# A two-layer streaming encoder on one core: the second output half of layer 0 done block by block, and the last attention queries no longer issued by force

## The chip, the core and the metric

The kernel runs on one core of one Trainium2 chip. The engines are named as in the profile: PE multiplies matrices (PEld is its weight load), DVE is the vector engine, ACT the scalar engine, POOL is GpSimd, and SP issues the transfers. The metric is the device time of one execution in microseconds (us), the median of several runs.

## What is computed

One step of an encoder with two layers over 2,048 prompt tokens and 8 samples of 16 tokens, all in float32, model width 1,024.

```python
# layer 0
z = rms_norm(h, norm_ab) @ w_in_ab      # a_q, a_k, a_v, a_g, b_qkv, b_g, b_beta, b_alpha
q, k = rms_norm per head of a_q, a_k
o_a = sliding-window attention(q, k, a_v, sinks) * silu(a_g)       # mixer A, 8 heads of 64
o_b = rms_norm(gated delta rule(conv(b_qkv), beta, g)) * silu(b_g) # mixer B, 4 heads of 128
y = h + concatenate([o_a, o_b]) @ w_out_ab
# layer 1
z = rms_norm(y, norm_c) @ w_in_c        # u and its gate, 1,024 columns each
mixed = per group of 256: ((trailing mean over 2/4/8/16) - u) @ w_grp_c * scale
out = y + (mixed * silu(gate)) @ w_out_c
```

The outputs are both hidden streams and the new caches: keys, values, delta-rule states, and histories of the convolution and of the pooled stream.

## The kernel before

**Tiles and passes.** The tokens are taken in four groups. Group 0 has four blocks of 128 prompt tokens and the block of the samples; groups 1 to 3 have four blocks each, 512 tokens. A group runs through both layers before the next begins. Every operand of a product is a pair of a high part and a low part, and one product takes three matmuls (high x high, low x high, high x low): L702 to L704 where a weight stands and the tokens stream past (`proj_fm`), L1281 to L1283 where a block of tokens stands (`tok_major`), L733 to L735 in `out_half`.

**Weights.** The plan of weights is a list. `weight()` hands out the next one and loads up to two ahead into three buffers called `w`, of 1 MB each (L448, a transfer from SP, `w<-wk`). In group 0 the weights come raw, into `wst`, and are split there: ACT casts the high part (L471), DVE and POOL subtract to get the low part (L475).

**What sets the order.** The code is one long program in which each product calls `tick(us)`. Ticks advance a planner's clock. Work is handed to that clock in three ways: `start(job)` starts a generator, which goes on each time the clock reaches the time that it yielded; `defer(DEF, fn)` issues a function 7.0 ticks later; and `queue` holds generators that are taken in turn. `finish(job)` runs a job to its end at once, `flush()` issues everything that is pending at once, and `drain()` empties the queue. What is issued is then ordered on each engine by the framework's scheduler, and each engine works through its own order.

**The last queries ahead of the gates.** `a_queries(jp)` (L1336 ff.) makes the attention queries of half the heads. For each block it makes a product with `tok_major`, normalizes it per head on ACT, DVE and POOL (`head_norm`; its last step is POOL's multiplication L1304/L1305, after POOL's power, L501), and defers `qcols`: four PE transposes into a `tp` tile (L1388), an ACT scaling (L1390) and a DVE subtraction (L1392). Behind the last block, `end` starts `a_attend(jp)` (L1396), whose four units per group make scores on PE (L1445, L1446), a row maximum on DVE, exponentials and scaling on ACT (`soft`, L1415 and L1423), transposes (L1459) and the product with the values (L1474 to L1476). After `a_queries(1)` come `drain()` and `flush()` (L1629, L1630), which issue whatever is pending, then `gates_early(0)` and `gates(1)`, both made of projections.

**The output of layer 0.** `out_half` is called twice per group in layer 0: first for the heads of half 0, then for half 1. Of a call there are four steps, two output halves `c` by two weights `kk`. The second call is `out_half(ops1, y1, normed, True)`: the first output half goes weight by weight over all blocks, the second block by block with two weights held. After a block's last product DVE adds it to the residual (L756), and `normed(b)` normalizes the row for layer 1: `norm_rows` (L537 ff.) squares one half on ACT (L526) and one on DVE (L528), POOL makes the power (L501), DVE scales (L545). After every second block a `cols` job goes into the queue: `norm_cols` (L547 ff.) transposes eight column tiles of two blocks on PE (L557), ACT casts the high part (L560), DVE subtracts for the low part (L561). The `tp` tiles have two buffers. `drain()` after the call issues what is left of it.

**The pool layer.** For the first group of channels (`gi == 0`) two weights of `u` are held, and each is taken in two halves of the tokens (matmuls of 256 columns); the two weights of the gate follow over all tokens at once (512 columns).

Of the kernel before, what the change touches and what calls it, by code (L numbers as in the profile page):

```python
# [9 lines left out]
AF = mybir.ActivationFunctionType  # L10
# [227 lines left out]
def hybrid_kernel(  # L238
# [138 lines left out]
    def flush():  # L377
        while pend:
            pend.pop(0)[1]()
# [300 lines left out]
    def group(gix, norm_job):  # L680
# [43 lines left out]
            drop(a)  # L724
            return [(h[:, i, 0:n], lo[:, i, 0:n]) for i in range(2)], [h, lo]

        def out_half(ops, y1, done=None, by_block=False):

            def products(pp, b, kk, wt):
                tk = slice(P * b, P * b + P)  # L730
                for k in range(2):
                    oh, ol = ops[2 * kk + k]
                    mm(pp, oh[:, tk], wt[0][:, k, :], start=(kk == k == 0), stop=False)  # L733
                    mm(pp, oh[:, tk], wt[1][:, k, :], start=False, stop=False)  # L734
                    mm(pp, ol[:, tk], wt[0][:, k, :], start=False, stop=(kk == k == 1))  # L735
                    tick(0.64)

            for c in range(2):

                if c and by_block:  # L740
                    ws = [weight() for _ in range(2)]
                    seq = [(b, kk, ws[kk]) for b in range(nb) for kk in range(2)]
                else:
                    seq = [(b, kk, None) for kk in range(2) for b in range(nb)]
                open_ = {}
                for b, kk, wt in seq:
                    if wt is None:
                        if b == 0:
                            cur = weight()
                        wt = cur  # L750
                    if kk == 0:
                        open_[b] = psum(("pj", "pj", "rc", "rc", "sc")[b])
                    products(open_[b], b, kk, wt)
                    if kk:
                        ysl = y1[b][:, 512 * c:512 * c + 512]
                        V.tensor_tensor(ysl, open_.pop(b), ysl, op=ALU.add)  # L756
                        if done is not None and c:
                            done(b)

        finish(norm_job)  # L760

# [864 lines left out]
                used.extend(u)  # L1626
                yield 1.2

        drain()  # L1629
        flush()  # L1630
        finish(st["B", 0], st["A", 0])
        gates_early(0)
        ops0, used0, ops1, used1 = [], [], [], []
        gs = gates(1)
        finish(st["B", 1])
# [23 lines left out]
        gain = slot([P, D])  # L1659
        Q.dma_start(gain, gains[:, D:])  # L1660

        def normed(b):
            nx[b] = slot([P, D])
            norm_rows(y1[b], nx[b], gain)
            if b % 2 or b == nb - 1:
                b0 = b - b % 2

                def cols():
                    yield 1.2
                    yield from norm_cols([nx[i] for i in range(b0, b + 1)], b0, xh, xl)  # L1670
                    drop(*[nx[i] for i in range(b0, b + 1)])

                queue.append(cols())

        out_half(ops1, y1, normed, True)
        drop(gain, *used1)
        drain()


        def pool_sums(gi, u3, ln0, su):  # L1680
# [22 lines left out]
        for gi in range(4):  # L1703
# [18 lines left out]
                uss.append(us)  # L1722

            if gi == 0:
                ws = [weight() for _ in range(2)]
                seq = [(d, w, [part]) for part in halves for d, w in enumerate(ws)]
            else:
                seq = [(d, None, None) for d in range(2)]
            for d, w, parts in seq:
                ut, ub, us = 2 * gi + d, ubs[d], uss[d]  # L1730
                for pp, t0, t1 in proj_fm(w, parts):
                    e = min(t1, Tp)
# [29 lines left out]
                    drop(pl)  # L1762

                pools.append(start(pooled(), 0.6))
            for d in range(2):
                for pp, t0, t1 in proj_fm():
                    silu2(act[:, d, t0:t1], pp)
            wh, wl = weight()
# [61 lines left out]
```

## Time and profile before

| | |
|---|---|
| median of 3 runs | 1918.76 us (1918.02 to 1921.17) |
| the profiled execution | 1920.49 us |
| its span, first to last instruction | 1918.6 us |
| PE, PEld busy | 1834.6 us (96%), 1601.5 us (83%) |
| DVE, ACT, POOL busy | 1205.8 us (63%), 722.2 us (38%), 494.6 us (26%) |
| mean granted PE clock | 0.986 of full speed |

Times in rows are microseconds from the span's start. "[2.93 <-POOL B L1305]" after an instruction means that its engine sat idle for 2.93 us before it, until POOL's write of a B tile at line 1305. In the view of waits a row gives the total, the number of times and the longest. In the view of windows PEclk is the granted clock, 1.00 for 2.4 GHz and 0.50 for 1.2 GHz.

### The profile page before, as it was taken

To read this page: it belongs to the slowest core of one execution; us is meant where nothing else is said; L and a number is where in the kernel's file an instruction comes from. 1 tells how busy PE (TensorE), PEld (TensorE's weight loads), DVE (VectorE), ACT (ScalarE), POOL (GpSimd) and SP (SyncE) were. 2 spreads that over 40 slices of the span, in tenths; PEclk is the share of its full clock that TensorE was granted. 3 is DMA by queue.
4 is the path that set the end of the run, shared out by engine and by line. 5 is a ranking of instruction groups with operands and counts; after the bars stand their busy time and mean duration, and the time that the engine had idled before them with its cause. 6 is when DMAs were issued, how large, how long until landed. Compare 5 with 4: busy or idle time off the path is not lost. (4 is left out here: it accounts for less than half of the span.)

```text
span 1918.6 us, 30851 instructions
## 1 busy us (share of the span) xinstructions
PE 1834.6 (96%) x11362; PEld 1601.5 (83%) x11362; DVE 1205.8 (63%) x3215; ACT 722.2 (38%) x1846; POOL 494.6 (26%) x628
## 2 busy tenths in 40 slices
PE   6999989999999999999999999999999999999999
PEld 5988878878997988787888988787888978787887
DVE  6797957555665697754345597664345697754342
ACT  4465336323332474441222474341222474441210
POOL 5633451423332413310012413210012413210000
PEclk9998989999999999999999999999999999999999
DMA  7433453655668533435467533435457533435454
GB/s 274 143 132 125 135 195 96 237 197 205 222 240 297 202 113 121 146 132 186 157 219 287 200 116 100 153 121 187 168 207 292 198 107 111 153 124 187 172 189 189
DMA packets 94578, 337.51 MB, mean 176 GB/s; under 512 B 35884, under 2 KB 44332, under 8 KB 64988
## 3 DMA queue, kind: packets, MB, share of 16 engines
q1 hardware_dynamic: 94428, 335.54, 50.0%
q8 instruction: 90, 1.47, 0.3%
q14 instruction: 60, 0.49, 0.1%
HBM read 256.93 MB, written 78.58 MB: 175 GB/s over the span
## 5 line engine op out<-in xcount | busy, mean ns | idle before, releaser
L702 PE MATMUL pj<-XH,w 128*128 128x512 f32 (+3 forms) x1488 | 544.1, 366 | 5.4 <-ACT cb L852 3.4
L703 PE MATMUL pj<-XL,w 128*128 128x512 f32 (+3 forms) x1488 | 534.1, 359 | 0.1
L704 PE MATMUL pj<-XH,w 128*128 128x512 f32 (+3 forms) x1488 | 533.7, 359 | 0.0
L702 PEld LDWEIGHTS pj<-XH,w 128*128 128x128 f32 x1488 | 284.1, 191 | 34.7 <-ACT cb L852 3.6
L704 PEld LDWEIGHTS pj<-XH,w 128*128 128x128 f32 x1488 | 283.5, 191 | 30.4 <-issue 0.2
L703 PEld LDWEIGHTS pj<-XL,w 128*128 128x128 f32 x1488 | 284.1, 191 | 28.9 <-issue 0.7
L475 POOL TENSOR_TENSOR w<-wst,w 128x640 fp32r<-128x640 f32 (+2 forms) x60 | 106.2, 1770 | 154.6 <-ACT w L471 150.9
L1281 PE MATMUL pj<-w,XH 128*128 128x256 f32 (+1 forms) x368 | 107.2, 292 | 0.3 <-DVE VL L1327 0.3
L1283 PE MATMUL pj<-w,XL 128*128 128x256 f32 (+1 forms) x368 | 104.7, 285 | 0.0
L1282 PE MATMUL pj<-w,XH 128*128 128x256 f32 (+1 forms) x368 | 104.5, 284 | 0.0
L756 DVE TENSOR_TENSOR A<-pj,A 128x512 f32<-128x512 f32 x40 | 27.6, 690 | 106.0 <-PE pj L735 106.0
L471 ACT CAST w<-wst 128x1024 fp32r<-128x1024 f32 (+1 forms) x60 | 61.2, 1020 | 52.5 <-PE sc L735 42.0
L715 DVE SCALAR_TENSOR_TENSOR A<-A,pj 128x512 f32<-128x512 f32 x36 | 24.7, 687 | 88.2 <-ACT A L714 88.2
L735 PE MATMUL rc<-w,B 128*128 128x512 f32 x200 | 78.0, 390 | 0.0
L735 PE MATMUL pj<-w,B 128*128 128x512 f32 x200 | 77.9, 390 | 0.0
L1688 DVE TENSOR_TENSOR B<-cb 128x526 f32<-128x526 f32 x32 | 22.7, 709 | 79.5 <-ACT cb L1733 74.3
L1281 PEld LDWEIGHTS pj<-w,XH 128*128 128x128 f32 x368 | 70.3, 191 | 1.8 <-DVE VL L1327 0.5
L1282 PEld LDWEIGHTS pj<-w,XH 128*128 128x128 f32 x368 | 70.2, 191 | 1.1 <-issue 0.5
L1283 PEld LDWEIGHTS pj<-w,XL 128*128 128x128 f32 x368 | 70.2, 191 | 0.0
L475 DVE TENSOR_TENSOR w<-wst,w 128x384 fp32r<-128x384 f32 (+2 forms) x60 | 49.1, 818 | 32.7 <-ACT w L471 32.6
L733 PE MATMUL rc<-w,B 128*128 128x512 f32 x176 | 69.4, 394 | 0.0
L733 PE MATMUL pj<-w,B 128*128 128x512 f32 x176 | 68.7, 390 | 0.0
(488 smaller groups left out, 4294.8 us busy)
## 6 DMA issues: line engine op xcount, KB each, us to landing
w<-wk SPq DMA_DIRECT2D x168, 1024.0 KB, 4.9
wk<-w SPq DMA_DIRECT2D x56, 1024.0 KB, 6.5
wst<-in_wts SPq DMA_DIRECT2D x56, 512.0 KB, 4.3
A<-in_x SPq DMA_DIRECT2D x22, 512.0 KB, 4.5
w<-wk SPq DMA_DIRECT2D x6, 1056.0 KB, 5.7
B<-in_x SPq DMA_DIRECT2D x12, 512.0 KB, 4.8
w<-wk SPq DMA_DIRECT2D x12, 512.0 KB, 3.2
out_y<-B SPq DMA_DIRECT2D x9, 512.0 KB, 3.4
```

Of the source, the lines that this page charges most:

```text
L471: S.copy(hi, st)
L475: eng.tensor_tensor(lo[:, a:b], st[:, a:b], f32(hi[:, a:b]), op=ALU.subtract)
L702: mm(pp[:, 0:w], wh[:, k, :], xh[:, k, t0:t1], start=(k == 0), stop=False)
L703: mm(pp[:, 0:w], wh[:, k, :], xl[:, k, t0:t1], start=False, stop=False)
L704: mm(pp[:, 0:w], wl[:, k, :], xh[:, k, t0:t1], start=False, stop=(k == KT - 1))
L715: V.scalar_tensor_tensor(dst, dst, 1.0, pp, op0=ALU.add, op1=ALU.mult)
L733: mm(pp, oh[:, tk], wt[0][:, k, :], start=(kk == k == 0), stop=False)
L735: mm(pp, ol[:, tk], wt[0][:, k, :], start=False, stop=(kk == k == 1))
L756: V.tensor_tensor(ysl, open_.pop(b), ysl, op=ALU.add)
L1281: mm(pp[:, 0:N], xh[:, k, tk], wh[:, k % 4, :], start=(k == 0), stop=False)
L1282: mm(pp[:, 0:N], xh[:, k, tk], wl[:, k % 4, :], start=False, stop=False)
L1283: mm(pp[:, 0:N], xl[:, k, tk], wh[:, k % 4, :], start=False, stop=(k == KT - 1))
```

## The change

There are four parts.

1. `drain()` and `flush()` no longer stand ahead of the gates; one `flush()` stands behind `gates_early(0)`. The `qcols` of the last blocks are issued when their 7 ticks are over, among the gates' projections.
2. `out_half` has a new mode, `ahead`: the first weight of the first output half goes over all blocks, then the other three weights are held together. Blocks 0 and 1 take their three remaining steps each at once, and blocks 2 and up go step by step. The third held weight goes into the buffer of the first weight.
3. In `normed` both squares are ACT's; the scaling is a started job that runs 1.9 ticks later, and the column transposes are started jobs 3.0 ticks later instead of entries of the queue. The `drain()` behind the call is gone.
4. In the pool layer at `gi == 0` three weights are held, both of `u` and the first of the gate. Each is taken in halves: all three for the first half of the tokens, which only waits for the columns of blocks 0 and 1, then all three for the second half. The gain row of the norm is dropped later.

```diff
--- before.py
+++ after.py
@@ -724,7 +724,9 @@
             drop(a)
             return [(h[:, i, 0:n], lo[:, i, 0:n]) for i in range(2)], [h, lo]
-        def out_half(ops, y1, done=None, by_block=False):
+        def out_half(ops, y1, done=None, by_block=False, ahead=False):
             def products(pp, b, kk, wt):
                 tk = slice(P * b, P * b + P)
@@ -734,6 +736,31 @@
                     mm(pp, oh[:, tk], wt[1][:, k, :], start=False, stop=False)
                     mm(pp, ol[:, tk], wt[0][:, k, :], start=False, stop=(kk == k == 1))
                     tick(0.64)
+            def add(pp, b, c):
+                ysl = y1[b][:, 512 * c:512 * c + 512]
+                V.tensor_tensor(ysl, pp, ysl, op=ALU.add)
+                if done is not None and c:
+                    done(b)
+            if ahead:
+                cur = weight()
+                open_ = {}
+                for b in range(nb):
+                    open_[0, b] = psum(("pj", "pj", "rc", "rc", "sc")[b])
+                    products(open_[0, b], b, 0, cur)
+                ws = [weight() for _ in range(3)]
+                steps = ((0, 1), (1, 0), (1, 1))
+                seq = [(b, i) for b in range(2) for i in range(3)]
+                seq += [(b, i) for i in range(3) for b in range(2, nb)]
+                for b, i in seq:
+                    c, kk = steps[i]
+                    if i == 1:
+                        open_[1, b] = psum(("sc", "pj", "pj", "rc", "rc")[b])
+                    products(open_[c, b], b, kk, ws[i])
+                    if kk:
+                        add(open_.pop((c, b)), b, c)
+                return
             for c in range(2):
@@ -752,10 +779,7 @@
                         open_[b] = psum(("pj", "pj", "rc", "rc", "sc")[b])
                     products(open_[b], b, kk, wt)
                     if kk:
-                        ysl = y1[b][:, 512 * c:512 * c + 512]
-                        V.tensor_tensor(ysl, open_.pop(b), ysl, op=ALU.add)
-                        if done is not None and c:
-                            done(b)
+                        add(open_.pop(b), b, c)
         finish(norm_job)
@@ -1626,10 +1650,9 @@
                 used.extend(u)
                 yield 1.2
-        drain()
-        flush()
         finish(st["B", 0], st["A", 0])
         gates_early(0)
+        flush()
         ops0, used0, ops1, used1 = [], [], [], []
         gs = gates(1)
         finish(st["B", 1])
@@ -1659,22 +1682,34 @@
         gain = slot([P, D])
         Q.dma_start(gain, gains[:, D:])
+        normings, colings = [], []
         def normed(b):
             nx[b] = slot([P, D])
-            norm_rows(y1[b], nx[b], gain)
+            ss = buf([P, 4, 2], "ss", 4)
+            for i in range(2):
+                junk = buf([P, 512], "t", NT)
+                S.activation(junk, y1[b][:, 512 * i:512 * i + 512], AF.Square, accum_out=ss[:, 0, i:i + 1])
+            rs = inv_rms(ss, 1)
+            def scaled():
+                yield 1.9
+                V.scalar_tensor_tensor(nx[b], y1[b], rs[:, 0:1], gain, op0=ALU.mult, op1=ALU.mult)
+            normings.append(start(scaled()))
             if b % 2 or b == nb - 1:
                 b0 = b - b % 2
-                def cols():
-                    yield 1.2
+                def cols(mine=normings[-1]):
+                    yield 3.0
+                    finish(mine)
                     yield from norm_cols([nx[i] for i in range(b0, b + 1)], b0, xh, xl)
                     drop(*[nx[i] for i in range(b0, b + 1)])
-                queue.append(cols())
-        out_half(ops1, y1, normed, True)
-        drop(gain, *used1)
-        drain()
+                colings.append(start(cols()))
+        out_half(ops1, y1, normed, ahead=True)
+        drop(*used1)
         def pool_sums(gi, u3, ln0, su):
@@ -1722,11 +1757,18 @@
                 uss.append(us)
             if gi == 0:
-                ws = [weight() for _ in range(2)]
+                ws = [weight() for _ in range(3)]
                 seq = [(d, w, [part]) for part in halves for d, w in enumerate(ws)]
             else:
                 seq = [(d, None, None) for d in range(2)]
             for d, w, parts in seq:
+                if gi == 0:
+                    finish(*(colings[0:1] if parts[0][0] == 0 else colings))
+                if d == 2:
+                    for pp, t0, t1 in proj_fm(w, parts):
+                        silu2(act[:, 0, t0:t1], pp)
+                    continue
                 ut, ub, us = 2 * gi + d, ubs[d], uss[d]
                 for pp, t0, t1 in proj_fm(w, parts):
                     e = min(t1, Tp)
@@ -1762,7 +1804,11 @@
                     drop(pl)
                 pools.append(start(pooled(), 0.6))
+            if gi == 0:
+                drop(gain)
             for d in range(2):
+                if gi == 0 and d == 0:
+                    continue
                 for pp, t0, t1 in proj_fm():
                     silu2(act[:, d, t0:t1], pp)
             wh, wl = weight()
```
**PE, around the end of `a_queries(1)`, group 1, before.** `pj_1591` is the product of the last query block, `pj_1605` the first projection of the gates; `tp_1600`, `tp_1601` and `tp_1602` are the query columns of blocks 1, 2 and 3, and `sc_1611` are scores of `a_attend(1)`.

```order
L1388 MATMUL tp_1593_8923<-first_72,B10_1559_8731 128x128 x4
...
L1283 MATMUL pj_1591_8907<-w_1536_8628,XL_75 128x256
L1388 MATMUL tp_1600_8961<-first_72,B10_1559_8731 128x128 x4
L1388 MATMUL tp_1601_8968<-first_72,B2_1560_8732 128x128 x4
L702 MATMUL pj_1605_8985<-XH_74,w_1561_8733 128x512
...
L1445 MATMUL sc_1611_8998<-KH_76,A3_1557_8729 128x256
...
L1446 MATMUL sc_1612_9005<-KL_77,A3_1557_8729 128x256
L1388 MATMUL tp_1602_8975<-first_72,B2_1560_8732 128x128 x4
L702 MATMUL pj_1605_8985<-XH_74,w_1561_8733 128x512
```
The query columns of blocks 1 and 2 stand side by side right behind the last product, the first scores three matmuls later, and block 3 behind them.

**The same place after the change.** `pj_1590` is the last query product, `pj_1601` and `pj_1614` the gates; `tp_1603`, `tp_1610` and `tp_1615` are blocks 1, 2 and 3; L1412 is L1388 before, L1469 is L1445.

```order
L1412 MATMUL tp_1592_8920<-first_72,B2_1558_8728 128x128 x4
...
L1307 MATMUL pj_1590_8904<-w_1531_8617,XL_75 128x256
L702 MATMUL pj_1601_8961<-XH_74,w_1560_8730 128x512
...
L704 MATMUL pj_1601_8961<-XH_74,w_1560_8730 128x512
L1412 MATMUL tp_1603_8971<-first_72,B2_1558_8728 128x128 x4
L702 MATMUL pj_1601_8961<-XH_74,w_1560_8730 128x512
...
L704 MATMUL pj_1601_8961<-XH_74,w_1560_8730 128x512
L1412 MATMUL tp_1610_9012<-first_72,B3_1559_8729 128x128 x4
```
Six projections stand ahead of block 1 and twelve more ahead of block 2; another six, four transposes of mixer B and six projections stand ahead of block 3 (`tp_1615`). The first score of `a_attend(1)` stands 153 rows behind the last query product, past triangular inverses of mixer B; before it stood six rows behind. In groups 2 and 3 the rows stand alike. In group 0 the columns of blocks 0 and 1 keep their place behind the same projections in both programs.

**PE, the second output half, group 1, after the change.** `w_1780` is the first weight, `w_1785`, `w_1787` and `w_1792` are the three held; `pj_1788`, `pj_1789`, `rc_1790`, `rc_1791` are the sums of the first output half of blocks 0 to 3.

```order
L737 MATMUL rc_1791_9957<-w_1780_9872,B2_1775_9824 128x512
L735 MATMUL pj_1788_9936<-w_1785_9902,B8_1777_9836 128x512
...
L735 MATMUL sc_1795_9977<-w_1787_9934,A4_1774_9823 128x512
...
L735 MATMUL pj_1789_9943<-w_1785_9902,B8_1777_9836 128x512
...
L735 MATMUL sc_1795_9977<-w_1792_9964,B8_1777_9836 128x512
...
L735 MATMUL rc_1790_9950<-w_1785_9902,B8_1777_9836 128x512
...
L557 MATMUL tp_1810_10054<-first_72,A1_1796_9991 128x128
```
Before, the four blocks of `w_1785` stood together, and only `w_1787` and `w_1792` alternated. Now `w_1792` is needed 23 matmuls behind the last use of `w_1780`, whose buffer it takes. The first transposes (`tp_1810`) stand behind 15 matmuls that follow block 1's last product; before, 9 stood between them, and the transposes of blocks 2 and 3 came behind the last product of all.

## Rows read from the trace of the kernel before

**Rows 1.** The page: busy time of the engines over the span.
```profile
PE 1834.6 (96%) x11362; PEld 1601.5 (83%) x11362; DVE 1205.8 (63%) x3215; ACT 722.2 (38%) x1846; POOL 494.6 (26%) x628
```
**Rows 2.** Waits of PE over the whole span, its first two.
```profile
PE tp L1388 <- POOL B L1305: 17.6, 10, 3.4
PE tp L557 <- DVE XL L561: 11.2, 8, 3.8
```
**Rows 3.** Timeline of group 1 at the last queries: start, duration, engine, line, operation.
```profile
776.89 0.60 PE L1388 MATMUL tp<-first,B 128*128 128x128 f32 x4
...
780.43 1.11 PE L1388 MATMUL tp<-first,B 128*128 128x128 f32 x4 [2.93 <-POOL B L1305]
...
783.68 0.61 POOL L1305 TENSOR_TENSOR B<-B,rsa 128x256 f32<-128x256 f32 x1
```
**Rows 4.** Waits of PE in 250:266, 774:786, 1200:1217 and 1636:1647, one row each.
```profile
PE tp L1388 <- POOL B L1305: 6.5, 4, 3.4
...
PE tp L1388 <- POOL B L1305: 3.2, 2, 2.9
...
PE tp L1388 <- POOL B L1305: 4.4, 3, 3.0
...
PE tp L1388 <- POOL B L1305: 3.4, 1, 3.4
```
**Rows 5.** Windows behind those waits: us, busy PE, PEld, DVE, ACT, POOL, PEclk, DMA, GB/s.
```profile
257.60:267.80 10.20, 8.18 (x34) 7.34 (x33) 6.05 (x10) 3.21 (x7) 7.74 (x10) 0.50 0.81 312
...
779.90:783.30 3.40, 2.87 (x11) 2.58 (x12) 3.27 (x8) 0.69 (x1) 1.79 (x3) 0.50 0.65 251
...
1209.90:1216.70 6.80, 5.99 (x21) 4.96 (x21) 5.79 (x15) 0.94 (x2) 3.11 (x5) 0.50 0.02 8
1640.00:1646.80 6.80, 5.65 (x21) 5.09 (x22) 5.10 (x10) 1.26 (x2) 3.25 (x5) 0.50 0.35 135
```
**Rows 6.** Window of the attention of group 0, columns as in rows 5.
```profile
287.20:320.00 32.80, 31.18 (x243) 28.23 (x242) 27.54 (x122) 25.34 (x82) 2.08 (x2) 1.00 0.26 81
```
**Rows 7.** Waits of PE in 890:920 (group 1, three rows), then in 415:450 (group 0).
```profile
PE tp L557 <- DVE XL L561: 1.5, 1, 1.5
PE tp L557 <- DVE A L545: 1.1, 1, 1.1
PE tp L557 <- DVE B L545: 0.4, 1, 0.4
...
PE tp L557 <- DVE XL L561: 2.8, 4, 1.2
PE tp L557 <- DVE B L545: 1.6, 2, 1.0
```
**Rows 8.** Timeline of group 1: matmuls of `out_half`, one block's addition and scaling.
```profile
889.72 0.39 PE L735 MATMUL rc<-w,B 128*128 128x512 f32 x1
...
894.03 0.39 PE L733 MATMUL pj<-w,B 128*128 128x512 f32 x1
...
894.90 0.69 DVE L756 TENSOR_TENSOR A<-pj,A 128x512 f32<-128x512 f32 x1 [2.03 <-PE pj L735]
...
897.45 1.28 DVE L545 SCALAR_TENSOR_TENSOR A<-A,rs,A 128x1024 f32<-128x1024 f32 x1 [0.67 <-POOL rs L501]
```
**Rows 9.** Timeline of group 1: matmuls of 256 columns in the pool layer.
```profile
916.05 0.28 PE L702 MATMUL pj<-XH,w 128*128 128x256 f32 x1
...
918.92 0.28 PE L702 MATMUL pj<-XH,w 128*128 128x256 f32 x1
```
**Rows 10.** Line L448 in 862:885: weight transfers of group 1's output.
```profile
DMA to landing us min/median/max: 4.7/4.8/6.5
```
**Rows 11.** Groups in 380:446, group 0: the split of a raw weight.
```profile
L471 ACT CAST w<-wst 128x1024 fp32r<-128x1024 f32 x8 | 8.4, 1050 | 29.2 <-PE sc L735 25.5 <-issue 3.7
...
L475 POOL TENSOR_TENSOR w<-wst,w 128x512 fp32r<-128x512 f32 x5 | 9.0, 1799 | 22.0 <-ACT w L471 22.0
```
**Rows 12.** Waits of PE in 786:846: group 1's attention, the one row.
```profile
PE sc L1057 <- ACT B L1050: 0.2, 1, 0.2
```
## The prediction

> **What bounds the kernel now.** I read the page first: PE is busy for 1834.6 us of the span and no other engine for more than 1205.8 [rows 1]. So PE sets the time, and an edit is worth what it takes out of PE's idle time or out of PE's slow stretches. The view of waits comes next. The longest wait is that of the query transposes L1388 for POOL's normalization L1305, 17.6 us, then that of the column transposes L557 of the second norm [rows 2]. Both are what the change touches.
>
> The timeline of group 1 shows how the first wait comes about. PE transposes one block's queries at 776.89 and is through at 777.49. The next transposes are already issued, by force, but POOL has not normalized that block, so PE sits for 2.93 us with projections ready behind it [rows 3]. The reader should see that it is a matter of PE's order: POOL's result for the last block ends at 783.68 + 0.61 = 784.3, 7.4 us after PE was through with its query products at 776.9, while projections that depend on nothing of this stand just behind. Split by group the wait is 6.5, 3.2, 4.4 and 3.4 us [rows 4]. Each of these is followed by a stretch at the lower clock: the granted clock is 0.50, which is 1.2 GHz, for 10.2 us in group 0 and for 3.4, 6.8 and 6.8 us in groups 1 to 3, with PE busy in them for 8.18, 2.87, 5.99 and 5.65 us [rows 5]. Before each fall PE had sat idle for 3 us or so.
>
> In the norm, PE waits 1.5 + 1.1 + 0.4 = 3.0 us in group 1 and 2.8 + 1.6 = 4.4 us in group 0 [rows 7]; groups 2 and 3 repeat group 1's three rows to 0.1 us, so groups 1 to 3 make 8.9 us. The reason is the chain behind a block's last product: DVE adds at 894.90, and the scaled row is there at 897.45 + 1.28 = 898.73 [rows 8], 3.8 us, about 4.4 with the product's own last 0.39 and the hand-over. The old order had little else for PE behind the last pair.
>
> **Part 1, no forced issue.** In groups 1 to 3 the order now has six projections ahead of block 1's query columns, twelve more ahead of block 2's, and the rest ahead of block 3's. From one matmul of 512 columns to the next it is (894.03 - 889.72) / 19 = 0.227 us [rows 8], nineteen steps lying between the two rows. Eighteen projections and one set of transposes of 0.60 us [rows 3] put block 2's at 18 x 0.227 + 0.6 = 4.7 us behind the query products; POOL's result for it came when PE went on at 780.43, 3.5 us behind them, and in groups 2 and 3 the longest waits are 0.1 and 0.5 us longer than group 1's [rows 4]. Block 3's stand at 4.7 + 0.6 + 12 x 0.227 + 0.6 (mixer B's transposes, taken as the query's) = 8.6 us, against 7.4 in group 1. So the waits of 3.2, 4.4 and 3.4 us go: **-11.0 us**, less a residual of 0.4 a group where DVE delays POOL (**+1.2**; the ends are 0 and the 11.0 itself). With the idle time goes the slow clock: half of the PE time in those three stretches, (2.87 + 5.99 + 5.65) / 2 = **-7.2 us**. In group 0 the columns of blocks 0 and 1 keep their place behind the same projections, so the wait of 6.5 us and the half of 8.18 behind it stay. I take 0; the other end is -10.6.
>
> The price is that the four attention units of the last queries are no longer begun early. Before, two were scored while DVE worked through mixer B's inverse, and PE lost only 0.2 us in all of the attention [rows 12]. Now all four run bunched behind the inverse. The trace has such a bunch, in group 0: in 32.8 us PE is busy for 31.18, DVE for 27.54 and ACT for 25.34, at clock 1.00 [rows 6]. PE idles there for 1.6 us, and I charge that to each of three groups: **+4.8**. The lower end is 0 (projections fill in), the upper end is the second rival. Group 0's own bunch was there before.
>
> The Trainium skill has a rule that speaks against this part ("TensorE: Matmul & The Clock Gate", section "A second HAM failure mode: psum-queue depth-cycling"): a PE that idles briefly and often between groups of matmuls makes the clock go back and forth between its levels. By that rule half of a bunch's 31.18 us might run at 1.2 GHz, 15.6 us more a group, and the sum would end near 1939. The trace disagrees: group 0's bunch is full of such short waits and keeps clock 1.00 [rows 6].
>
> **Parts 2 and 3, the output by blocks and the norm.** No product is added. The first pair's transposes now stand behind 15 more matmuls, 3.4 us, and a set of block 2's, where the scaled row takes 4.4; the second pair's columns are needed only by the second half of the pool layer's tokens, 72 matmuls of 256 columns after the last product. From one of these to the next it is (918.92 - 916.05) / 24 = 0.12 us [rows 9], so that is 8.6 us of cover. Of 8.9 us in groups 1 to 3 I leave 0.4 a group: **-7.7**. In group 0, with five blocks and splits on ACT and POOL, I leave 1.5 of 4.4: **-2.9**. The ends are no gain and the whole 13.3. Moving the second square from DVE to ACT costs PE nothing as long as the chain is covered so; uncovered, ACT's second square would add about the 0.69 us that DVE's took.
>
> Holding three weights costs lookahead. The third is loaded only when the first is done with, and is needed 23 matmuls later: 23 x 0.227 = 5.2 us, against a landing of 4.8 us in the median and 6.5 at worst [rows 10]. The spare in the median is 0.4 us. I take **+0.3** for three groups, from 0 to 1.3 each. In group 0 the weight has been loaded but must be split: ACT 1.05 and POOL 1.80 us [rows 11], about 3.1 with the hand-overs, behind two products of 6 x 0.227 x 2 = 2.7: **+0.5**, from 0 to 3.
>
> **Part 4, the pool layer.** The three weights go into the buffers of the three held before, in the order in which these come free. The last is free at the last product and needed 48 matmuls of 256 columns later, 5.7 us against 4.8: nothing, and 0.8 a group at the worst landing. The gate's first weight now takes 48 matmuls of 256 columns instead of 24 of 512: 48 x 0.12 = 5.7 for 5.4 us, so 0.23 a group: **+0.7** in all. The gain row dropped later costs a buffer, not time.
>
> **Sum.** -11.0 - 7.2 + 1.2 + 4.8 - 7.7 - 2.9 + 0.3 + 0.5 + 0.7 = -21.3 us. The profiled execution took 1920.5 us, 1.7 above the median of the runs; from it the sum gives 1899.2, and from the median of 1918.8 it gives **1897.5**.
>
> **The rivals.**
> - *The wait moves but half of it stays.* If DVE, busy with the inverse, delivers the sums of squares to POOL a few us later than now, the transposes still come before their data. For it: the waits end at POOL's last step, but POOL itself idles before that. Against it: nothing is put ahead of these sums on DVE. Half of 11.0 and 7.2 given back makes 9.1: 1906.6.
> - *Slower: the bunch is limited by the softmax.* ACT and DVE work in order, and ACT needs 25.34 / 4 = 6.3 us for a unit [rows 6]. If PE had other work for only 3.8 us of these, it would wait 2.5 us four times, 10 us a group, and lose the clock behind as in rows 5, 7.2 / 3 = 2.4 us. That is 12.5 for 1.6 a group: 1897.5 - 4.8 + 37.5 = 1930. It decides from (21.3 + 4.8) / 3 = 8.7 us a group. For it: the early scores are gone, and unlike in group 0 the two layers' other waits are short, so any new one shows. Against it: group 0's own bunch, and the gates' projections that stand between its matmuls.
> - *Better: group 0 gains too and the bunch is free.* Without the 4.8, and with group 0's 10.6: 1882. Against it: group 0's order at that place is nearly unchanged.
>
> That the change doesn't do what it says applies to group 0 alone, and is in the sum.
>
> **How the numbers follow.** A measurement of this kernel can tell about 0.2%, 3.8 us, from no change. I give the forecast 0.68, the first rival 0.15, the slower one 0.11 (of it 0.07 above 1922.6 and 0.03 within 0.2%), the better one 0.06. Of the first rival 0.02 may end within 0.2%. So faster is 0.88, the same 0.05, slower 0.07. The range goes from 1882, the better rival, to 1911, the first rival with the worst landings (3 x 1.3); it leaves out the slower rival and the tails, less than 0.2.
>
> **What would show it.** Right: in the view of waits L1388 for POOL falls from 17.6 to about 8, nearly all in group 0; the windows behind the queries of groups 1 to 3 show PEclk 1.00, and only group 0 keeps a stretch at 0.50; L557's waits fall to some 3 us; a wait on a weight's transfer in `out_half` is under 0.5 us a time. Wrong: PE waiting for ACT or DVE at the scores, transposes or value products of `a_attend(1)` for more than 3 us a group, or a new stretch at clock 0.50 there or at the third held weight.

## The result and the profile after

The changed kernel takes 1899.91 us in the median (1898.98 to 1901.78), against 1919.28 us (1918.02 to 1921.17) before in the same measurement: 19.4 us less, ratio 0.9898 with a 95% interval of 0.9885 to 0.991. The prediction was 1897.5, with a range of 1882 to 1911. The profiled execution of the changed kernel took 1898.98 us and has a span of 1897.2, 21.4 us under that of before.

The page's busy times of the changed kernel answer to [rows 1], and the first waits of PE over the whole span to [rows 2]. Lines have moved: L1412 is L1388 before, L1329 is L1305, L1287 is L1263, L1697 is the scaling L545.

```profile
PE 1824.5 (96%) x11434; PEld 1598.7 (84%) x11434; DVE 1196.4 (63%) x3184; ACT 733.8 (39%) x1883; POOL 498.8 (26%) x628
...
PE tp L592 <- POOL rs L501: 11.2, 4, 8.3
PE tp L1412 <- POOL B L1329: 6.0, 3, 3.4
PE tp L1412 <- DVE A L1416: 5.6, 3, 1.9
PE tp L557 <- DVE A L1697: 4.6, 6, 1.1
...
PE tp L557 <- DVE B L1697: 2.2, 2, 1.9
...
PE tp L1287 <- DVE A L1416: 2.0, 3, 0.7
```

The wait for POOL has fallen from 17.6 to 6.0 us, and what is left of it is group 0's. A new pair stands in its place: 5.6 + 2.0 us for DVE's line L1416. The wait of L557 for DVE's subtraction (11.2 us) is down to the 3.8 of the start of the kernel, and waits for the scaling L1697 remain, 4.6 + 2.2 us.

The windows at the queries answer to [rows 5]; columns as there. The second row is another place, the norm of group 0.

```profile
256.70:263.50 6.80, 5.24 (x23) 4.80 (x22) 4.80 (x8) 2.52 (x6) 6.49 (x8) 0.50 0.98 398
...
434.20:437.60 3.40, 3.40 (x18) 3.40 (x17) 2.48 (x3) 0.98 (x2) 0.21 (x1) 0.50 0.81 336
...
776.00:785.00 9.00, 6.46 (x34) 4.87 (x33) 8.57 (x20) 1.98 (x3) 2.45 (x3) 1.00 0.41 152
...
1200.00:1210.00 10.00, 7.42 (x38) 5.66 (x37) 9.53 (x22) 1.98 (x3) 2.44 (x4) 1.00 0.45 167
1624.00:1634.00 10.00, 7.53 (x38) 5.72 (x37) 9.50 (x21) 2.21 (x4) 3.54 (x5) 1.00 0.58 211
```

Group 0 still has a stretch at clock 0.50, of 6.8 us instead of 10.2. It has a new one besides, of 3.4 us behind the 1.9 us that PE waits at the norm's column transposes; before there was none at that place. In groups 1 to 3 there is none: PEclk is 1.00, though PE idles for 2.5 us in each of these windows.

Where the time went, by stage, from the starts of the first query columns of the second half (L1388, now L1412) and of the first output product (L733, now L735) to the last output product of the pool layer:

| stage | queries to output, before | after | output to end of pool layer, before | after |
|---|---|---|---|---|
| group 0 | 253.0 to 371.5 = 118.5 | 252.2 to 368.1 = 115.9 | 371.5 to 624.0 = 252.5 | 368.1 to 618.9 = 250.8 |
| group 1 | 775.0 to 858.4 = 83.4 | 769.9 to 851.3 = 81.4 | 858.4 to 1052.7 = 194.3 | 851.3 to 1044.3 = 193.0 |
| group 2 | 1202.5 to 1288.7 = 86.2 | 1194.4 to 1275.7 = 81.3 | 1288.7 to 1483.7 = 195.0 | 1275.7 to 1469.2 = 193.5 |
| group 3 | 1635.1 to 1720.1 = 85.0 | 1619.6 to 1700.1 = 80.5 | 1720.1 to 1913.4 = 193.3 | 1700.1 to 1892.0 = 191.9 |

The first stage lost 2.6 + 2.0 + 4.9 + 4.5 = 14.0 us, the second 1.7 + 1.3 + 1.5 + 1.4 = 5.9. The other 1.5 us lie in stages that the change leaves alone.

### The profile page after: what moved, and what is told of

It reads as the page before. It is cut to its first block, busy times and chain, and to the rows that moved or that the text cites. A ratio compares the mean times of both kernels' runs of the same rounds, so it can differ in the third digit from the quotient of the medians.

```text
span 1897.2 us, 30999 instructions
## 1 busy us (share of the span) xinstructions
PE 1824.5 (96%) x11434; PEld 1598.7 (84%) x11434; DVE 1196.4 (63%) x3184; ACT 733.8 (39%) x1883; POOL 498.8 (26%) x628
## 4 chain that ended last, share of the span: by engine, by line
PE 74%; DVE 16%; POOL 3%; issue 3%; ACT 2%; DMA 2%; SPq 0%; DVEq 0%; POOLq 0%; ACTq 0%
PE pj L702 12%; PE pj L704 12%; PE pj L703 12%; PE pj L737 3%; PE pj L735 3%; PE pj L736 3%; PE rc L737 2%; PE rc L735 2%; PE rc L736 2%; DVE tm L1019 2%; DVE A L1020 2%; PE pj L1305 2%; PE pj L1306 2%; PE pj L1307 2%; PE tp L557 1%
## 5 line engine op out<-in xcount | busy, mean ns | idle before, releaser
L702 PEld LDWEIGHTS pj<-XH,w 128*128 128x128 f32 x1512 | 288.2, 191 | 33.7 <-ACT cb L876 3.7
L704 PEld LDWEIGHTS pj<-XH,w 128*128 128x128 f32 x1512 | 287.5, 190 | 29.3 <-issue 0.2
L703 PEld LDWEIGHTS pj<-XL,w 128*128 128x128 f32 x1512 | 288.0, 190 | 26.5 <-issue 0.2
L1305 PE MATMUL pj<-w,XH 128*128 128x256 f32 (+1 forms) x368 | 106.8, 291 | 0.3 <-DVE VL L1351 0.3
L737 PE MATMUL pj<-w,B 128*128 128x512 f32 x224 | 87.5, 391 | 0.0
L737 PE MATMUL rc<-w,B 128*128 128x512 f32 x212 | 82.6, 390 | 0.0
L715 DVE SCALAR_TENSOR_TENSOR A<-A,pj 128x512 f32<-128x512 f32 (+1 forms) x33 | 21.1, 639 | 80.1 <-ACT A L714 79.8
L1305 PEld LDWEIGHTS pj<-w,XH 128*128 128x128 f32 x368 | 70.0, 190 | 1.7 <-DVE VL L1351 0.5
L1019 DVE TENSOR_TENSOR tm<-A,A 40x31 f32<-40x31 f32 (+31 forms) x155 | 62.9, 406 | 6.8 <-DMA A<-Ld 4.4
L896 DVE SCALAR_TENSOR_TENSOR B<-cb,taps,B 128x512 f32<-128x512 f32 x78 | 57.8, 741 | 11.9 <-ACT B L885 11.2
```

The lines of the kernel that those rows point to most:

```text
L702: mm(pp[:, 0:w], wh[:, k, :], xh[:, k, t0:t1], start=(k == 0), stop=False)
L703: mm(pp[:, 0:w], wh[:, k, :], xl[:, k, t0:t1], start=False, stop=False)
L704: mm(pp[:, 0:w], wl[:, k, :], xh[:, k, t0:t1], start=False, stop=(k == KT - 1))
L1019: V.tensor_tensor(t3, bc(Lb[:, j + 1:32, j], w), bcm(Xb[:, j, 0:w], r), op=ALU.mult)
L1305: mm(pp[:, 0:N], xh[:, k, tk], wh[:, k % 4, :], start=(k == 0), stop=False)
```

## The experiments

Two theories stood against each other at each place: that PE's order alone was at fault, so that a later place in the order wins the wait for good, and that behind the wait stands another engine, so that the wait moves.

**Part 1 alone, and the rest alone.** First the kernel before with part 1:

```diff
-        drain()
-        flush()
         finish(st["B", 0], st["A", 0])
         gates_early(0)
+        flush()
```

> The kernel before with part 1 alone: the forced issue ahead of the gates is gone, out_half, the norm and the pool layer are as before. Theory (the terms of the sum add up): from the first query columns of the second half to the first output product, groups 1 to 3 lose 2.0 + 4.9 + 4.5 = 11.4 us between the two profiles, so about -11 us, 1908 of 1919.3, without any stretch at clock 0.50 behind the queries of groups 1 to 3, and with waits of 0.6 and 1.8 us a group on DVE's subtraction. Rival (the parts lean on each other, and the bunched attention is only harmless because the new output follows it): less than -6 us, above 1913, with waits of PE on ACT or DVE in the attention of 2 us a group or more.

Measured: 1907.24 us (1906.88 to 1907.77) against 1919.79, ratio 0.9937 (0.9922 to 0.9952), 12.6 us less, as the theory has it but for one stretch at the lower clock behind group 3's queries, which was not to be there. Then the changed kernel with the same two lines put back:

> The changed kernel with the forced issue put back ahead of the gates: parts 2, 3 and 4 alone. Theory: what lies behind the first output product lost 1.3 + 1.5 + 1.5 us in groups 1 to 3 and 1.7 in group 0 between the two profiles, so about -6 us, 1913 of 1919.3; the waits of 17.6 us on POOL's normalization and the four stretches at clock 0.50 are back. Rival (the forced issue hurts the new order, or the reverse): the difference to the changed kernel is not the 11 us of part 1 but under 8 or over 16.

Measured: 1914.80 us (1914.0 to 1917.84), ratio 0.9978 (0.9969 to 0.9988), 5.0 us less, and 14.9 over the changed kernel: between the theory's 11 and the rival's bound of 16. The parts add up to within 2 us: 12.6 + 5.0 = 17.6 of 19.4. The first waits of PE over the whole span in the first of the two kernels, whose line numbers are those of before, and its stretch in group 3:

```profile
PE tp L557 <- DVE XL L561: 11.2, 8, 3.8
...
PE tp L1388 <- POOL B L1305: 6.3, 4, 3.4
PE tp L1388 <- DVE A L1392: 5.5, 3, 1.9
PE tp L557 <- DVE A L545: 4.0, 4, 1.1
...
1637.80:1641.20 3.40, 3.40 (x10) 2.63 (x9) 3.27 (x8) 0.69 (x1) 0.00 (x0) 0.50 0.00 0
```

The norm's waits are those of before, and the wait on DVE's subtraction (L1392 here) is there without the new output. It is part 1's own. In the kernel with the forced issue the wait for POOL is back in full, with two of the three slow stretches of groups 1 to 3 (the one of group 1 did not come in that execution):

```profile
PE tp L1412 <- POOL B L1329: 19.0, 9, 3.4
...
779.00:786.00 7.00, 5.25 (x30) 4.51 (x31) 5.58 (x12) 1.38 (x2) 3.19 (x6) 1.00 0.18 71
1207.60:1214.40 6.80, 5.79 (x20) 4.72 (x20) 5.83 (x15) 0.69 (x1) 3.10 (x5) 0.50 0.03 11
1637.60:1641.10 3.50, 3.32 (x13) 3.03 (x14) 3.37 (x8) 0.69 (x1) 1.81 (x4) 0.51 0.51 215
```

**The new wait.** The timeline of the changed kernel at the queries of group 1 shows what it is (start, duration, engine, line, operation):

```profile
776.41 0.60 PE L1412 MATMUL tp<-first,B 128*128 128x128 f32 x4
...
777.05 0.69 ACT L1414 ACTIVATE A<-tp,gq 128x512 fp32r<-128x512 f32 x1 [2.51 <-PE tp L1412]
...
779.61 0.71 DVE L1020 TENSOR_TENSOR A<-A,tm 32x252 f32<-32x252 f32 x1
...
782.10 0.76 DVE L1416 SCALAR_TENSOR_TENSOR A<-tp,gq,A 64x512 fp32r<-64x512 f32 x1
...
783.00 0.63 PE L1412 MATMUL tp<-first,B 128*128 128x128 f32 x4 [1.91 <-DVE A L1416]
```

Block 2's columns are in their `tp` tile at 777.0, and ACT has read them by 777.74. DVE reads them last, in L1416, and comes to that only at 782.10, behind steps of mixer B's inverse (L1019, L1020). Block 3 needs the tile and waits until 783.00. DVE read as late before the change. There PE transposes the columns of block 0 at 775.02 and those of block 1 at 776.89 [rows 3], and DVE reads them at 779.04 and 781.85:

```profile
775.02 0.60 PE L1388 MATMUL tp<-first,B 128*128 128x128 f32 x4
...
779.04 0.76 DVE L1392 SCALAR_TENSOR_TENSOR A<-tp,gq,A 64x512 fp32r<-64x512 f32 x1
...
781.85 0.76 DVE L1392 SCALAR_TENSOR_TENSOR A<-tp,gq,A 64x512 fp32r<-64x512 f32 x1
```

With two buffers these are the tiles that blocks 2 and 3 need next. They were free at 779.80 and 782.61, and PE went on at 780.43 and 784.35, when POOL was through: the wait for POOL hid the one for DVE.

The next kernel takes the query columns to other tiles:

```diff
                 def qcols(z=z, b=b):
-                    pt = psum("tp")
+                    pt = psum("rc")
```

> The changed kernel with the query columns in the rc tiles of PSUM instead of tp. In the changed kernel PE waits 0.6 and 1.9 us a group at the query columns until DVE's subtraction has read the tp tile of the block before last. Theory A (the tile is held, because the subtraction stands late in DVE's order behind steps of mixer B's inverse): with other tiles both waits go in groups 1 to 3, 7.6 us in all, about 1892. Theory B (DVE is the limit there and whatever follows waits for the same work): the waits turn up at the next use of the rc tiles or at the scores, and the time stays within 2 us of the changed kernel's 1899.9.

Measured: 1897.03 us (1894.93 to 1900.05), ratio 0.988 (0.9863 to 0.9896): 2.9 us under the changed kernel, not 7.6. The 2.5 us a group are gone at the queries, but the waits of PE now have a row for a transfer, and behind it stand new stretches at the lower clock in two groups. The trace is of the slowest of the four runs, 1900.05 us:

```profile
PE sc L1046 <- DMA A<-Xd: 4.0, 3, 2.1
...
803.05 0.67 PE L1046 MATMUL sc<-A,B 32*32 32x32 f32 x16 [1.54 <-DMA A<-Xd]
...
803.60:807.00 3.40, 3.40 (x12) 2.68 (x9) 0.00 (x0) 0.37 (x1) 0.00 (x0) 0.50 0.77 308
1230.20:1233.70 3.50, 3.50 (x15) 2.76 (x13) 0.00 (x0) 0.37 (x1) 0.00 (x0) 0.51 0.68 281
```

The transfer carries the blocks of the inverse that DVE has made back from memory (`Xd`). In the changed kernel PE takes them at 802.43 without a wait, and the last of these transfers was issued at 799.6 and takes 2.8 to 3.4 us, so it lands just about then. The time is between the theories. The mechanism is theory B's in part: DVE's inverse is the next thing that PE needs, and of the 7.6 us won at the queries 4.0 are spent waiting for it, with the slow clock behind. In this trace the stage from the queries to the output is no shorter in groups 1 and 2 (81.5 and 81.9 us) and 2.1 us shorter in group 3 (78.4), where the clock did not fall. Group 0, whose queries moved to the `rc` tiles too, is 2.9 us longer over both stages.

**Group 0.** Here the wait for POOL had stayed.

```diff
-                defer(DEF, qcols)
+                defer(DEF + (6.0 if samp and jp else 0.0), qcols)
...
-            defer(DEF + 0.1, end)
+            defer(DEF + (6.0 if samp and jp else 0.0) + 0.1, end)
```

> The changed kernel with the query columns of the second half deferred by 6 more ticks in group 0 alone. In the changed kernel group 0 still waits 1.1 + 3.4 + 1.6 us for POOL there, and 6.8 us run at clock 0.50 behind it. Theory (it is PE's order there too): the wait falls to 1 to 2 us and the slow stretch goes, 4.5 + 3.4 = about -8 us, 1892. Rival (POOL is behind because of the weights that it splits in group 0, and the attention that starts later costs as much): the waits move to the later columns or to the scores, and less than 3 us are gained.

Measured: 1895.84 us (1894.13 to 1899.59), ratio 0.988 (0.9865 to 0.9894), 4.1 us under the changed kernel, between the two. The waits of PE in 250:275 and two windows:

```profile
PE tp L1287 <- DVE A L1416: 3.2, 1, 3.2
PE tp L1412 <- POOL B L1329: 1.4, 2, 1.1
...
252.00:263.00 11.00, 7.44 (x52) 6.94 (x53) 9.33 (x19) 4.52 (x10) 10.53 (x14) 1.00 0.66 226
263.00:275.00 12.00, 12.00 (x102) 11.77 (x100) 5.95 (x10) 3.94 (x7) 4.93 (x5) 1.00 0.79 240
```

POOL's share falls from 6.0 to 1.4 us and the clock stays at 1.00, but 3.2 us of wait have turned up at mixer B's transposes L1287, which need the `tp` tile that DVE has not read. It is the same new wait as in the other groups. Over both stages group 0 is about 6 us shorter; in group 2 the clock fell behind the wait of 1.91 us at the queries, for 3.4 us, and that stage is 1.6 us longer.

**The norm.** Three kernels ask which part of the remaining 1.5 us a group is order and which is the chain. The first starts the columns later:

```diff
-                    yield 3.0
+                    yield 4.2
                     finish(mine)
```

> The changed kernel with the column transposes of the second norm started 4.2 ticks instead of 3.0 after the second row of a pair. In the changed kernel PE waits there 0.46 and 1.08 us a group in groups 1 to 3 and 0.36 and 1.9 us in group 0, for DVE's scaling. Theory A (only PE's order is wrong by about a microsecond): the waits go, 3 x 1.5 + 2.2 = 6.8 us at most, about 1894. Theory B (the chain behind the last row is what the pool layer's second half waits for): the waits move to the column products of the pool layer and less than 2 us are gained.

Measured: 1898.20 us (1897.58 to 1900.43), ratio 0.9889 (0.9875 to 0.9904): 1.7 us less, within the scatter and within theory B's bound. The waits of a group fell from 1.5 to 1.0 us, and no row of PE's waits shows the rest elsewhere. The second gives DVE its square back:

```diff
-            for i in range(2):
-                junk = buf([P, 512], "t", NT)
-                S.activation(junk, y1[b][:, 512 * i:512 * i + 512], AF.Square, accum_out=ss[:, 0, i:i + 1])
+            squares(y1[b], ss[:, 0, :])
```

> The changed kernel with the second square of the norm back on DVE. Theory A (the two squares in a row on ACT lengthen the chain): the scaled rows come 0.6 us earlier and the waits of 1.54 us a group fall to about 0.5, 3 us less, 1897. Theory B (the square on DVE stands between the additions and the scalings of the neighbouring block and costs what it saves): within 1.5 us of 1899.9.

Measured: 1897.87 us (1897.46 to 1898.16), ratio 0.9886 (0.9869 to 0.9902): 2.0 us less, between the two theories and near the scatter. In the trace the waits of a group fell from 1.5 to 0.6 us, with none above 0.35 us in groups 1 to 3, and the stage from the output on is 2.8 us shorter in these groups: 192.2, 192.2 and 191.2 against 193.0, 193.5 and 191.9. That is theory A's size; a slow stretch of 3.4 us at group 1's queries took 1.6 us of it back in that execution. So the two squares in a row on ACT, which I had costed at nothing while the chain is covered, made the chain longer where it was not covered. The third undoes part 3 whole: `norm_rows` again, `queue.append(cols())`, `drain()` behind the output, no `finish(*colings...)` in the pool layer.

> The changed kernel with part 3 undone: the norm as before, its column jobs in the queue and a drain behind the output, and the pool layer no longer waits for single column jobs; parts 1, 2 and 4 stay. Theory A (the new order of the products, part 2, carries the gain behind the first output product): 1899 to 1902, with waits at the column transposes of 1 to 2 us a group. Theory B (the jobs of part 3 carry it): the waits of 3 us a group and 4.4 in group 0 are back, 1903 to 1906.

Measured: 1900.58 us (1899.39 to 1902.0), ratio 0.9902 (0.9887 to 0.9916), no difference from the changed kernel that can be told. Part 3 as a whole neither gives nor takes; its two pieces do. The stage from the output on is 193.0, 193.7 and 191.9 us here in groups 1 to 3, as in the changed kernel, and 3.0 us shorter in the kernel with the jobs and DVE's square (e6). So the jobs win about 3 us, and the second square on ACT loses about as much. What the changed kernel gains behind the first output product is then left to the order of the products, part 2; no run has part 2 alone.

**The pool layer.** Part 4 undone:

```diff
-                ws = [weight() for _ in range(3)]
+                ws = [weight() for _ in range(2)]
...
-                if gi == 0 and d == 0:
-                    continue
                 for pp, t0, t1 in proj_fm():
```

> The changed kernel with part 4 undone but for the waits on the column jobs: two weights held in the pool layer, so 48 matmuls of 256 columns (5.7 us) instead of 72 (8.6 us) stand between the last output product and the first product that needs the columns of blocks 2 and up. Theory A (the longer cover is needed, since the columns are only through some 10 us behind the last product): PE waits 2 to 3 us a group for the columns, 1906 to 1911. Theory B (the cover is more than is needed): the wait is under 0.5 us a group and the matmuls of 512 columns give back 0.2, 1899 to 1901.

Measured: 1899.35 us (1898.39 to 1901.8), ratio 0.9895 (0.988 to 0.991). Theory B: 48 matmuls are cover enough, and part 4 is worth nothing that can be told either way.

**How near is the bunched attention to the softmax's limit?**

```diff
             for i in range(k):
+                if twice:
+                    junk = buf([P, 512], "t", NT)
+                    S.activation(junk[:, 0:nk], sP[:, i, 0:nk], AF.Exp, bias=mn[:, i:i + 1],
+                                 scale=over[0][i] if over else 1.0)
                 S.activation(sP[:, i, 0:nk], sP[:, i, 0:nk], AF.Exp, bias=mn[:, i:i + 1],
```

> The changed kernel with each exponential of the last queries' attention computed twice on ACT, the first time into a tile that nobody reads: 16 more of 0.50 us, 8 us of ACT a group. It measures how near the bunched attention is to being limited by the softmax, the slower rival's mechanism. Forecast's theory (PE has projections to do): under 2 us a group, below 1908. Rival's theory (ACT is busy for 9.3 of 10 us in the middle of the bunch, so it is at the edge): 4 to 8 us a group of waits of PE on ACT or on DVE behind it, 1916 to 1932.

Measured: 1946.50 us (1945.1 to 1949.63), ratio 1.0141 (1.0126 to 1.0156): 46.6 us over the changed kernel, more than either theory gave, and by another way than either. The waits of PE in group 1 (790:850), with the timeline's row and the windows around it:

```profile
PE sc L1046 <- DMA A<-Xd: 6.2, 1, 6.2
PE tp L1412 <- DVE A L1416: 1.9, 1, 1.9
...
PE sc L1502 <- ACT pT L1490: 0.2, 1, 0.2
...
801.13 0.39 PE L704 MATMUL pj<-XH,w 128*128 128x512 f32 x1
807.73 1.49 PE L1046 MATMUL sc<-A,B 32*32 32x32 f32 x28 [6.21 <-DMA A<-Xd]
...
805.60:822.70 17.10, 13.62 (x136) 12.15 (x137) 7.34 (x29) 7.23 (x22) 0.74 (x2) 0.50 0.28 70
822.70:850.00 27.30, 27.06 (x188) 24.42 (x187) 19.89 (x77) 25.45 (x76) 1.84 (x3) 1.00 0.21 68
```

PE hardly waits for ACT there: 0.2 us, although ACT is busy for 25.45 of 27.30 us in the second window. It waits for the inverse's transfer. In the changed kernel's order 106 matmuls of projections stand between the last query product and the inverse's first products; in this kernel's, which the scheduler made with the longer ACT work in it, 72 do. That is 34 x 0.227 = 7.7 us less cover. So 6.2 to 6.8 us of wait appear in each of groups 1 to 3, and 17 to 20 us at clock 0.50 behind each. As a measure of the softmax the run is spoiled, since a PE at half clock is easier for ACT to keep up with. What it shows is another thing: what the cover of the inverse's transfer is worth. The 19.2 us of waits for it and half of PE's time in the three slow stretches, (13.6 + 16.4 + 15.2) / 2 = 22.6, are 41.8 of the 46.6 us. Group 0 has no such wait, and there the run may say something of the softmax: its stage from the queries to the output is 6.0 us longer (122.0 for 116.0), within the rival's 4 to 8, and PE's longest waits in 285:325 are on DVE and ACT, the second and third of them in the attention:

```profile
PE pj L702 <- DVE t L715: 1.3, 1, 1.3
PE sc L1473 <- DVE mx L1477: 0.9, 1, 0.9
PE sc L1502 <- ACT pT L1490: 0.7, 1, 0.7
```

How much twice the exponentials would cost the other groups stays open.

**What adds up.** The late queries of group 0 and the square on DVE together:

> The changed kernel with the late query columns of group 0 (as in e4) and the second square on DVE (as in e6). If the two are separate, their gains add: 1899.9 - 4.1 - 2.0 = 1893.8. If not (the time won ahead of group 0's output is lost to it again, as a part of e4's was), 1895 to 1897.

Measured: 1893.77 us (1892.97 to 1898.46), ratio 0.9871 (0.9856 to 0.9886), the sum of the two. And with the query columns of groups 1 to 3 in the `rc` tiles:

```diff
-                    pt = psum("tp")
+                    pt = psum("tp" if samp else "rc")
```

> e9 with the query columns of groups 1 to 3 in the rc tiles as well (as in e3, but not in group 0). Theory A (e3 lost to its changes in group 0): the 2.5 us a group come on top, 7.5 us under e9. Theory B (the next thing that PE needs is the inverse's transfer through memory, which lands about a microsecond before PE takes it now): at most 1 us a group on top, and in the trace PE waits 1.5 to 2 us a group for that transfer, in some groups with a stretch at clock 0.50 behind it, so 0 to 3 us under e9.

Measured: 1890.97 us (1888.32 to 1893.62), ratio 0.9856 (0.9839 to 0.9872), the lowest median of the study, 8.9 us under the changed one and 28.6 under the one before, and 2.8 under e9, whose runs it overlaps. Its wait for the inverse is there, 3.1 us in two groups where theory B had 1.5 to 2 in each of three, and this time, in the fastest of the four runs, without a slow stretch.

```profile
PE sc L1046 <- DMA A<-Xd: 3.1, 2, 1.6
```

## Why the prediction was right

The sum was -21.3 us, and the profiled executions differ by 21.5 (1920.49 to 1898.98). The medians differ by 19.4. That the sum comes so near is partly luck: its terms miss by up to 6.4 us, some each way. By its steps:

- *PE sets the time, and the change takes out idle time and slow stretches.* Right: 19.9 of 21.4 us lie in the two stages of the rows of before.
- *The waits for POOL in groups 1 to 3 go, -11.0, less 0.4 a group.* The waits for POOL went, as said. The residual was mis-sized: 7.6 us for three groups instead of 1.2. The step said that DVE might delay POOL; what delays PE is DVE's own reading of the `tp` tile, L1416, which the sum did not look at. It could have been read from the trace of before, where DVE reads the tiles 4 to 5 us after PE begins to write them (779.04 for 775.02, 781.85 for 776.89) and the wait for POOL covers it.
- *The slow clock goes, -7.2.* Right for the profiled execution: no stretch at 0.50 behind the queries of groups 1 to 3. It is not sure in each: e1, e4, e6 and e11, with the same waits there, have one of 3.4 us each, and that group's stage is 1.6 to 2.3 us longer than in the changed kernel.
- *The bunched attention costs 1.6 us a group, +4.8.* Too much. A window over the bunch of group 1 in the changed kernel, columns as in [rows 6]:

```profile
810.00:845.00 35.00, 34.62 (x257) 30.34 (x256) 26.31 (x111) 28.68 (x87) 4.33 (x7) 1.00 0.31 105
```

PE is busy for 34.62 of 35.00 us. Group 0's bunch was too dear a model for the others. The two misses, 6.4 us too little for the residual and 4.8 too much here, nearly cancel, which is luck: the step was to give 11.0 + 7.2 - 1.2 - 4.8 = 12.2 us in groups 1 to 3, and it gave 2.0 + 4.9 + 4.5 = 11.4.
- *Group 0's queries: nothing.* It was 2.6 us: the wait is nearly the same (6.5, now 6.0), but the slow stretch behind it is 3.4 us shorter, worth about 1.7. Part 1 alone has it too (254.0 to 369.6 = 115.6 us for that stage). Its length varies: e5 and e7, alike at that place, have 3.4 us where the changed kernel has 6.8.
- *The norm: -7.7 and -2.9.* The residual was 1.5 us a group instead of 0.4; with the square on DVE it is 0.6 (e6), so ACT's second square made the chain longer than the 4.4 us that I took from before; with part 4's and the weights' terms the step was to give 6.7 in groups 1 to 3 and gave 1.3 + 1.5 + 1.4 = 4.2. In group 0 it was to give 2.4 with the split's term and gave 1.7; the wait fell from 4.4 to 2.2 us, and the new slow stretch behind it takes half of its 3.4 us. L557's waits in the norm were to fall to some 3 us; they are 4.6 + 2.2.
- *The third held weight: +0.3, from 0 to 1.3 each.* The transfers of the output's weights in group 1 land like the first row, where [rows 10] had 6.5 at worst. PE itself does not wait for them; its weight load does once, in the second row. In group 0 (+0.5) the weight load waits once for the split, in the third:

```profile
DMA to landing us min/median/max: 4.8/4.8/4.9
...
PEld sc L735 <- DMA w<-wk: 0.3, 1, 0.3
...
PEld sc L736 <- POOL w L475: 0.5, 1, 0.5
```
- *Part 4: +0.7.* 5.7 less 5.4 is 0.3 a group, not 0.23, so the term was to be +0.9. The run without part 4 (e7) differs by 0.6 us, which can't be told from nothing.

- *The rivals.* Of the wait more than the first rival's half stayed in size (7.6 of 11.0), but for another reason: it ends at DVE's reading and not at POOL's step. The slow clock did not stay with it in the profiled execution, and the time is 6.7 us under the rival's 1906.6. The slower one, the softmax, did not happen. The Trainium skill's rule in "TensorE: Matmul & The Clock Gate", section "A second HAM failure mode: psum-queue depth-cycling", would have had the clock go back and forth in the bunch; the granted clock there is 1.00. The evidence against it in the prediction was thinner than it says: group 0's bunch before had not many short waits but four in the view, 1.3 us in all.

## What to carry to other kernels

A wait that a forced issue puts in PE's order is worth more than its length where the clock falls behind it, so look at the windows that follow a wait before costing it. When a wait goes by moving its instruction, ask for every resource that instruction holds in its new place: here the PSUM tile, which is free only when the slowest reader in its own queue has come to it. Look for that reader in the trace of before, too, where a longer wait may cover it. And find the next transfer that the won time runs into: the order that hides a wait also hides the one behind it, and both an extra 2.5 us in hand (e3) and 7.7 us less cover (e8) showed up at the same instruction.

## What the runs showed of the hardware that was not expected

How long PE sat idle does not by itself tell whether the clock falls. Nine executions (the changed kernel, e1, e4 to e9 and e11) have a wait of 1.8 to 1.9 us at the queries in each of groups 1 to 3. Of these 27 waits 23 left the clock at 1.00; it fell behind one each in e1, e4, e6 and e11. In e3 it fell to 0.50 behind waits of 1.54 and 2.10 us; in e10 it stayed at 1.00 behind 1.62 and 1.44 us at the same instruction. Group 0's wait of 3.2 us at L1287 left it at 1.00 in e4 and e10, and it fell behind it in e9. The same place of group 1 kept its clock behind 3.39 us of wait in e2, where before it had fallen behind 2.93. A gain that rests on one such stretch is therefore not sure in each execution. The four runs of e3 lie between 1894.93 and 1900.05 us, with a mean granted clock of 0.989 in the slowest and 0.991 in the others; that such stretches make this spread is not shown.
